# A hybrid SSD and stick-breaking trunk on one core: the key's split one step later, the last two attention units multiplied before either is added, and the form products behind the third sum

## The chip, the core and the metric

The kernel runs on one core of a Trainium2 chip. A core has a matrix engine (TensorE; PE in the rows, with PEld for its weight loads), a vector engine (DVE), an activation engine (ACT), a fourth engine for simple work on tensors (POOL), and a queue from which most transfers are issued (SP). Each engine executes its own instructions in order and waits on semaphores for the others. The metric is the device time in microseconds (us) of one launch.

## The reference, cut to what matters

The model is a two-layer trunk on 1024 tokens of width 1024, with 16 learned tokens in front (1040 in all). Layer 0 is a state-space mixer and a convolutional feed-forward network (FFN). Layer 1 is stick-breaking attention with 16 heads of 64, and another FFN.

```
h = concat(meta_tokens, x)
h = h + ssd_mixer(rmsnorm(h));   h = h + conv_ffn(rmsnorm(h))          # layer 0
k, v = split(rmsnorm(h) @ w_kv); q = rmsnorm(h) @ w_q
logits = q k^T / 8;  visible = s < t
log_keep = where(visible, log_sigmoid(-logits), 0)
later    = reverse_cumsum(log_keep) - log_keep
w        = exp(where(visible, log_sigmoid(logits) + later, -inf))
h = h + (w @ v) @ w_o;           h = h + conv_ffn(rmsnorm(h))          # layer 1
out = rmsnorm(h)[16:]
conv_ffn(u) = (silu(g) * val) @ w_down,   g, val = split(dwconv3(u @ w_up))
```

## The kernel before

**Numbers as two parts.** Every large product is made of three matmuls (L209, L210, L211): a float32 operand is split into a high part (rounded by a copy on ACT) and a low part (the difference, mostly on DVE or POOL). A "split" below is such a copy and such a difference.

**Attention.** Heads are worked in 8 pairs. A pair's keys, queries and values are projected (tile `pj`) in three token tiles of 348, 348 and 344. For a pair there are 18 steps n = 0 to 17, each a block of at most 116 queries (i, 0 to 8) against one tile of keys (jj). In the order of the code they are i = 0, 1, 2 with jj = 0 (n = 0 to 2); i = 3, 4, 5 with jj = 1, then 0 (n = 3 to 8); i = 6, 7, 8 with jj = 2, 1, 0 (n = 9 to 17). So step 9 is the first that reads key tile 2, and its logits are the first after step 3 that are only 116 columns wide.

A step does this. PE multiplies queries and keys (`lg`, L1653, into a tile of two PSUM banks of which there is one). ACT takes two sigmoids of it (`kp` L1654, `bt` L1655). DVE scans `kp` (L1664) and multiplies into `bt` (L1665). Two steps later PE transposes `bt` (`wT`, L1687), ACT copies that out (`wt`, L1693), and when a visit is complete PE multiplies it with the values (`po`, L1710); ACT and DVE split the result (L1713, L1714), and it goes to DRAM.

While pair p is in its steps, the projections of pair p+1 and the rest of pair p's own are spread over them by the table `halves` in `attention`: key tile 2 of the pair itself is projected in steps 4 and 5, key tile 0 of the next pair in steps 8 and 9, key tile 1 of the next in steps 14 and 15. `half` multiplies the finished key by its token factors on DVE at once (L1577) and returns a list of calls for the step after (`late`, then `todo`). For a key that call is `key`: the copy on ACT (L1588), the difference `klo` on DVE (L1589), and three transfers on SP (L1590 to L1592) that move halves of the two parts to other partitions, so that a query can meet both parts. PE, DVE, ACT and POOL execute the attention in the order in which the code issues it.

**The output projection** of the first 4 pairs begins in the last pair: units of 12 matmuls (`acc`), each followed by an add to the residual on DVE (L538). After the last step two units are taken from a two-bank tile (`both`, named `acc` too), the others from single banks.

**Entering an FFN.** `enter_ffn` finishes the residual, makes a factor per token (L993 to L999), and `forms` makes sums and differences of quarters of the normalised residual, split into parts: the products with the factors on DVE (L1091), differences on DVE (`ft`, L1115), the copies on ACT (`bh`, L1097) and the differences on DVE (`bl`, L1098). These are the operands of a product in 7 instead of 8 multiplications, `up`. Of the second half of the tokens the forms are made while `up` multiplies the first block of weights (b = 0) with the first half. In that block three sums are formed (L1237), the third being `add(z, z, u2)` at the end of the third step. Outside the attention a scheduler sets each engine's order from the dependencies and a simulated time, with some orders tied by hand through `behind`.

Of the kernel before, what the change touches and what calls it, by code (L numbers as in the profile page):

```python
# [105 lines left out]
class Trunk:  # L106
    def __init__(self, ctx, tc, a):
        self.tc, self.nc, self.a = tc, tc.nc, a
        nc = self.nc
        self.cp = ctx.enter_context(tc.tile_pool(name="cp", bufs=1))  # L110
        self.qp = ctx.enter_context(tc.tile_pool(name="qp", bufs=NQ))
        self.tmps = ctx.enter_context(tc.tile_pool(name="up", bufs=8))
        self.wp = ctx.enter_context(tc.tile_pool(name="wp", bufs=3))
        self.mp = ctx.enter_context(tc.tile_pool(name="mp", bufs=2, space=bass.MemoryType.PSUM))
        self.sp = ctx.enter_context(tc.tile_pool(name="sp", bufs=SMB, space=bass.MemoryType.PSUM))
        self.dp = ctx.enter_context(tc.tile_pool(name="dp", bufs=1, space=bass.MemoryType.DRAM))
        self.lp = None
        self.n = 0
        self.open = []
        self.hold = self.copy_tie = self.silu_tie = None  # L120
        self.consts()


# [404 lines left out]
    def accumulate(self, h, f, s0, n, w, ks, front=0, bank=None, base=0, new=False):  # L528

        ps = (bank or (self.ex if f % 3 == 2 else self.mm))("acc")  # L530
        c, o = slice(s0 - base, s0 - base + n), slice(front + s0, front + s0 + n)
        for i, (hi, lo) in enumerate(ks):
            wh, wl = w(i, f)
            self.mm3(ps[:, :n], wh, wl, hi[:, c], lo[:, c], i == 0, i == len(ks) - 1)
        if new:
            self.nc.vector.tensor_copy(h[f][:, o], ps[:, :n])
        else:
            self.nc.vector.tensor_tensor(h[f][:, o], h[f][:, o], ps[:, :n], op=ALU.add)  # L538

# [535 lines left out]
    def forms(self, layer, h, r, t, tiles, pool):  # L1075


        nc, gain, FN = self.nc, f"ffn_norm{layer}", FFN[layer].tile
        N, N2 = HB + FN, HB + 2 * FN
        K = range(KD // 2)  # L1080
        out, own, wide = tiles
        s = slice(2 * FN * t, 2 * FN * t + N2)

        new = slice(s.start + HB * t, s.stop)
        b1, b2 = [h[k][:, s] for k in K], [h[k + KD // 2][:, s] for k in K]
        b11, b12, b21, b22 = [[b[:, c] for b in rows] for rows in (b1, b2) for c in (slice(0, N), slice(FN, N2))]

        def product(ks, part):
            c = slice(new.start, s.start + N) if part == 0 else slice(s.start + N, new.stop)
            for k in ks:  # L1090
                nc.vector.scalar_tensor_tensor(h[k][:, c], h[k][:, c], self.par(gain, k), r[:, c], op0=ALU.mult, op1=ALU.mult)  # L1091

        last = [self.after_factors, None]

        def parts(hls, xs):
            for hl, x in zip(hls, xs):
                hi = nc.scalar.activation(hl[0], x, AF.Copy)  # L1097
                low = nc.vector.tensor_tensor(hl[1], x, hl[0].bitcast(F32), op=ALU.subtract)  # L1098
                if t:
                    self.behind(hi, last[0], "behind the factors and the form in front")  # L1100
                    self.behind(low, last[1], "behind the form in front")
                    last[:] = hi, low
            self.last_high, self.last_low = hi, low

        def form(i, xs):
            own(i)
            parts(out[i], xs)

        def columns(tiles, xs, c):
            return [tuple(x[:, c] for x in hl) for hl in tiles], [x[:, c] for x in xs]  # L1110

        def minus(xs, ys, place=None):
            place = place or [self.ft(pool)[:, :N] for _ in K]
            for o, x, y in zip(place, xs, ys):
                nc.vector.tensor_tensor(o, x, y, op=ALU.subtract)  # L1115
            return place

        product(K, 0)
        if t:
            product(range(KD // 2, KD), 0)  # L1120
            yield
            product(K, 1)
            yield
            t1 = minus(b12, b11)
            product(range(KD // 2, KD), 1)
            yield
            t2 = minus(b22, t1)
            form(0, b11)
            both = wide()
        else:  # L1130
            yield
            form(0, b11)
            product(range(KD // 2, KD), 0)
            yield
# [66 lines left out]
    def up(self, layer, w0, forms, rest, pool):  # L1201
# [8 lines left out]
        def block(b, t, w, late=None):  # L1210

            def product(i, ps, start=True):
                wh, wl, c0 = w[i]
                for k in range(KD // 2):
                    c = slice(c0 + k * P, c0 + k * P + P)
                    self.mm3(ps[:, :N], wh[:, c], wl[:, c], *forms[t][0][i][k], start and k == 0, k == KD // 2 - 1, not start, self.after_sums if late is not None and i and k == 0 else None)
                return ps

            def conv(x, i, c):
                o = self.tmp("c")
                self.conv(x, o[:, :FN], FN, 3, HB, lambda q: self.par(cw, (KF * i + b) * 3 + q), self.par(cb, KF * i + b), tie=None if late is None else self.first_low)
                if i == 0:
                    nc.scalar.activation(o[:, :FN], o[:, :FN], AF.Silu)
                return o

            def done(g, v, j):
                self.last_up = tt(g[:, :FN], g[:, :FN], v[:, :FN], op=ALU.mult)
                nc.sync.dma_start(d[b, :, FN * j : FN * j + FN], g[:, :FN])  # L1230

            def copy(ps):
                s = self.ft(pool)
                nc.scalar.activation(s[:, :N], ps[:, :N], AF.Copy)  # L1234
                return s

            add = lambda o, x, y: tt(o[:, :N], x[:, :N], y[:, :N], op=ALU.add)  # L1237
            x = product(0, self.mm("p"))
            p1 = copy(x)
            yield  # L1240
            y = product(2, self.sm("p"))
            add(y, y, p1)
            u2 = copy(y)
            yield
            z = product(3, (self.ex if next(turn) else self.lg)("p"))
            p5 = copy(z)
            add(z, z, u2)
            yield
            made = {}
            run = (lambda f: f()) if late is None else late.append  # L1250
            product(1, x, False)
            run(lambda: made.update(g0=conv(x, 0, 0)))
            yield
            u3 = copy(product(4, y, False))
            run(lambda: (add(p5, p5, u3), made.update(v1=conv(p5, 1, 1))))
            yield
            product(5, z, False)
            run(lambda: done(conv(z, 0, 1), made["v1"], 2 * t + 1))
            yield
            product(6, y, False)  # L1260
            run(lambda: done(made["g0"], conv(y, 1, 0), 2 * t))
            yield
# [252 lines left out]
    def heads(self, u, p, pool):  # L1515
# [4 lines left out]
        class Pair:  # L1520
# [38 lines left out]
            def half(me, kind, j, h, bank=None, parts=2):  # L1559
# [15 lines left out]
                t = self.tmp(kind)  # L1575
                if kind == "k":
                    nc.vector.tensor_tensor(t[:, :n], ps[:, :n], u[KD][:, o:e], op=ALU.mult)  # L1577
                    return [lambda: me.key(j, t)]
                nc.scalar.activation(t[:, :n], ps[:, :n], AF.Copy)
                me.late.append((j, t))  # L1580
                return []
# [137 lines left out]
    def attention(self, u, pool, hd):  # L1719
# [34 lines left out]
        for kind, j, bank in (("k", 0, self.mm), ("q", 0, self.mm), ("k", 1, self.sm), ("q", 1, self.ex)):  # L1754
            for h in range(2):
                for f in first.half(kind, j, h, bank):
                    f()
            if (kind, j) == ("k", 0):
                self.late_factors()
        self.token_factors(u[KD], pool)  # L1760
        for p in range(PAIRS):
            prev = None
            for n, (i, jj) in enumerate(steps):
# [14 lines left out]
                for own, pair in now.items():  # L1778
                    if p + 1 < PAIRS and (own, n) in halves:
                        late += pair.half(*halves[own, n])  # L1780
                for f in todo + chores[:1]:
                    f()
                del chores[:1]
                for own, pair in now.items():
# [4 lines left out]
        both = self.lg2("acc")  # L1789
        banks = iter([lambda s, a=a: both[:, a] for a in range(2)])  # L1790
        self.unit_bank = lambda s: next(banks, self.mm)(s)
        while turns or ready:
            next(behind)
            next(behind)
            flush(0)
        return od, behind

# [260 lines left out]
```

## Time and profile before

| | |
|---|---|
| three runs | 2851.83, 2857.06, 2860.83 us, median 2857.06 |
| the profiled execution | 2855.13 us, of which the span of instructions is 2853.3 |
| busy in the span | PE 2809.2, DVE 2065.4, ACT 1580.2, POOL 1578.6 us |
| attention, pair 0's first logits to the last add | about 1539 to 2061 us, some 65.2 us a pair |
| forms of the second half | about 838 to 862 us in layer 0, 2164 to 2191 us in layer 1 |
| mean granted clock of the matrix engine | 0.997 |

A row of the timeline has the start, the length, engine, line, operation, tiles (out <- in), shape and count, and in brackets the idle time of the engine just before it with what ended it. A row of waits has the waiting engine and line, the line waited for, the total, the count and the longest. A row of a window has its length, then for PE, PEld, DVE, ACT and POOL the busy time with the count of instructions, then the granted clock of the matrix engine, the busy share of the transfer engines and GB/s. Tiles' buffer numbers are left out in the profile.

### The profile page before, as it was taken

What the parts mean: (1) busy time and instruction counts of PE and PEld (TensorE: products, weight loads), DVE (VectorE), ACT (ScalarE), POOL (GpSimd) and SP (SyncE); (2) the same over time, 40 slices, a digit from 0 to 9 for tenths busy, and PEclk for the clock granted to TensorE, in tenths of its full rate; (3) what the DMA queues carried; (4) which work ended last, traced back from release to release, by engine and by line L of the source; (5) the groups of instructions that cost most, each with busy time, mean ns of one, the idle gap of its engine ahead of it and who ended that gap; (6) DMA issues with size and microseconds to landing.
All of it is one profiled execution on the core that took longest, in us unless ns stands there. A gap on an engine that the chain in (4) does not pass through costs nothing.

```text
span 2853.3 us, 56464 instructions
## 1 busy us (share of the span) xinstructions
PE 2809.2 (98%) x21251; PEld 2691.9 (94%) x21251; DVE 2065.4 (72%) x3936; ACT 1580.2 (55%) x3077; POOL 1578.6 (55%) x2144
## 2 busy tenths in 40 slices
PE   8999999999999999999999999999999999999998
PEld 7989999999999999999999999999899999999888
DVE  5676666668487676767886888888749676766776
ACT  5554554543256555555335777777536555555433
POOL 2366455553519888867763212112254888886881
PEclk9999999999999999999999999999999999999999
DMA  4333333343413222235142222222532222225331
GB/s 119 86 112 93 121 83 125 116 136 101 120 64 96 78 80 78 79 135 176 49 142 77 74 73 69 80 70 57 184 131 77 82 80 82 75 82 185 111 104 67
DMA packets 141740, 281.78 MB, mean 99 GB/s; under 512 B 16307, under 2 KB 71740, under 8 KB 141468
## 3 DMA queue, kind: packets, MB, share of 16 engines
q1 hardware_dynamic: 135844, 267.01, 29.8%
q0 software_dynamic: 2048, 6.49, 0.6%
q10 hardware_dynamic: 3576, 4.67, 0.5%
q8 instruction: 168, 2.75, 0.4%
q14 instruction: 104, 0.85, 0.1%
HBM read 207.79 MB, written 55.42 MB: 92 GB/s over the span
## 4 chain that ended last, share of the span: by engine, by line
PE 91%; DVE 4%; ACT 2%; POOL 1%; issue 1%; DMA 0%; SPq 0%; ACTq 0%; DVEq 0%; POOLq 0%
PE p L209 10%; PE p L210 10%; PE p L211 10%; PE acc L209 8%; PE acc L211 8%; PE acc L210 8%; PE pj L209 8%; PE pj L210 8%; PE pj L211 8%; PE po L1710 3%; PE lg L1653 2%; PE wT L1687 2%; PE y L810 1%; PE S L799 1%; PE y L812 1%; PE ms L1069 1%
## 5 line engine op out<-in xcount | busy, mean ns | idle before, releaser
L102 POOL TENSOR_TENSOR wl<-w,wh 128x256 fp32r<-128x256 f32 x760 | 678.9, 923 | 352.2 <-ACT wh L196 225.4
L209 PE MATMUL pj<-uh,wh 128*128 128x348 f32 (+2 forms) x1536 | 500.4, 326 | 2.1 <-DVE xbc L339 1.4
L210 PE MATMUL pj<-ul,wh 128*128 128x348 f32 (+2 forms) x1536 | 494.9, 322 | 0.8 <-DVE ul L320 0.8
L211 PE MATMUL pj<-uh,wl 128*128 128x348 f32 (+2 forms) x1536 | 492.0, 320 | 0.0
L209 PE MATMUL p<-bh,fh 128*128 128x262 f32 (+1 forms) x1408 | 400.9, 285 | 3.9 <-DVE p L1237 3.7
L211 PE MATMUL p<-bh,fl 128*128 128x262 f32 (+1 forms) x1408 | 401.0, 285 | 0.9 <-POOL fl L102 0.9
L210 PE MATMUL p<-bl,fh 128*128 128x262 f32 (+1 forms) x1408 | 399.2, 284 | 0.0
L102 POOL TENSOR_TENSOR fl<-x,fh 128x256 fp32r<-128x256 f32 x352 | 264.3, 783 | 186.8 <-ACT fh L1174 160.9
L210 PE MATMUL p<-bl,wh 128*128 128x262 f32 (+1 forms) x1040 | 295.6, 284 | 1.1 <-DVE bl L1098 1.1
L209 PE MATMUL p<-bh,wh 128*128 128x262 f32 (+1 forms) x1040 | 295.3, 284 | 0.4 <-ACT ft L1234 0.4
L211 PE MATMUL p<-bh,wl 128*128 128x262 f32 (+1 forms) x1040 | 294.1, 283 | 0.0
L209 PEld LDWEIGHTS pj<-uh,wh 128*128 128x128 f32 x1536 | 288.7, 188 | 4.5 <-ACT xbc L336 1.7
L210 PEld LDWEIGHTS pj<-ul,wh 128*128 128x128 f32 x1536 | 289.2, 188 | 2.4 <-DVE ul L320 1.4
L211 PEld LDWEIGHTS pj<-uh,wl 128*128 128x128 f32 x1536 | 288.7, 188 | 0.1
L339 DVE SCALAR_TENSOR_TENSOR c<-p,params,c 128x260 f32<-128x260 f32 (+1 forms) x528 | 248.4, 480 | 54.7 <-ACT c L336 48.3
L209 PEld LDWEIGHTS p<-bh,fh 128*128 128x128 f32 x1408 | 268.0, 191 | 4.7 <-DVE p L1237 4.1
L211 PEld LDWEIGHTS p<-bh,fl 128*128 128x128 f32 x1408 | 267.1, 190 | 1.6 <-POOL fl L102 1.5
L210 PEld LDWEIGHTS p<-bl,fh 128*128 128x128 f32 x1408 | 267.8, 190 | 0.5 <-DVE bl L1098 0.4
L1234 ACT ACTIVATE ft<-p 128x262 f32<-128x262 f32 (+1 forms) x352 | 133.2, 382 | 179.9 <-DVE p L1237 110.1
L210 PE MATMUL acc<-gl,wh 128*128 128x260 f32 (+1 forms) x672 | 214.2, 320 | 0.0
L211 PE MATMUL acc<-gh,wl 128*128 128x260 f32 (+1 forms) x672 | 213.2, 319 | 0.0
L209 PE MATMUL acc<-gh,wh 128*128 128x260 f32 (+1 forms) x672 | 210.8, 320 | 0.1
(336 smaller groups left out, 7690.6 us busy)
## 6 DMA issues: line engine op xcount, KB each, us to landing
w<-in_w_up SPq DMA_DIRECT2D x88, 512.0 KB
w<-in_w_down SPq DMA_DIRECT2D x44, 512.0 KB
w<-in_w_in SPq DMA_DIRECT2D x40, 512.0 KB
E<-ea_d SPq DMA_DIRECT2D x32, 464.0 KB
D<-acs_d SPq DMA_DIRECT2D x32, 420.5 KB
g<-c SPq DMA_DIRECT2D x88, 130.0 KB
g<-c SPq DMA_DIRECT2D x88, 128.0 KB
b<-g SPq DMA_DIRECT2D x16, 520.0 KB
```

What stands on the lines that cost most here:

```text
L102: done.append(eng.tensor_tensor(out[:, c], x[:, c], y[:, c], op=op))
L209: self.behind(mm(out, wh, uh, start=first, stop=False, skip_group_check=joins), tie, "behind the sums of squares")
L210: mm(out, wh, ul, start=False, stop=False, skip_group_check=joins)
L211: self.last_mm = mm(out, wl, uh, start=False, stop=last, skip_group_check=joins)
L339: ins = nc.vector.scalar_tensor_tensor(out, ps[:, o + i : o + i + n], wcol(i), out, op0=ALU.mult, op1=ALU.add)
L799: nc.tensor.matmul(ps, bk[:n], xde[:n].rearrange("p h d -> p (h d)"), start=True, stop=True)
L810: nc.tensor.matmul(y, xdt[:n, i, :], dk[:, i, :], start=True, stop=c == 0)
L812: nc.tensor.matmul(y, state[:, i, :], ce[:, i, :], start=False, stop=True)
L1234: nc.scalar.activation(s[:, :N], ps[:, :N], AF.Copy)
L1653: nc.tensor.matmul(ps[:nt, a, :m], part[:, c0 : c0 + nt], ks[a][:, s0 : s0 + m], start=x == 0, stop=x == 1)
L1687: nc.tensor.transpose(pt[:ns, x * CB : x * CB + nt], bt[:nt, a, x * CB : x * CB + ns], self.ident[:nt, :nt])
L1710: nc.tensor.matmul(po[64 * a : 64 * a + 64, t0:n], v[: CH[c][1], c, 64 * a : 64 * a + 64], wt[a][q][: CH[c][1], r, t0:n], start=x == 0, st ...
```

## The change

Three edits.

1. In `half`, the call that a key returns gives back another call instead of doing the work, and the loop over steps appends what a call returns to `late`. So `key` (ACT copy, DVE difference, three transfers) is done one step later: in step 7 for key tile 2 of the pair's own (step 3 in the last pair), in step 11 and in step 17 for the next pair's tiles 0 and 1. The token-factor product L1577 stays.
2. In the loop that ends the attention, the adds of the first two units are collected and issued after both units' matmuls.
3. In the second half's `forms`, the products of the rows K..2K with the last factors are issued one step later, and tied behind the third sum of `up`, which now remembers it; since the order of the scheduler is then weighed anew, the first half of these products, which have no tie, and the following differences move with them.

```diff
@@ accumulate
+        elif self.adds is not None:
+            self.adds.append(lambda: self.nc.vector.tensor_tensor(h[f][:, o], h[f][:, o], ps[:, :n], op=ALU.add))
@@ forms
-        def product(ks, part):
+        def product(ks, part, tie=None):
             c = slice(new.start, s.start + N) if part == 0 else slice(s.start + N, new.stop)
             for k in ks:
-                nc.vector.scalar_tensor_tensor(h[k][:, c], ...)
+                ins = nc.vector.scalar_tensor_tensor(h[k][:, c], ...)
+                self.behind(ins, tie, "behind the third sum")
@@
             product(K, 1)
             yield
+            yield
+            product(range(KD // 2, KD), 1, self.third_sum)
             t1 = minus(b12, b11)
-            product(range(KD // 2, KD), 1)
-            yield
             t2 = minus(b22, t1)
@@ up, block
-            add(z, z, u2)
+            self.third_sum = add(z, z, u2)
@@ heads, half
-                    return [lambda: me.key(j, t)]
+                    return [lambda: [lambda: me.key(j, t)]]
@@ attention
-                for f in todo + chores[:1]:
+                for f in todo:
+                    late += f() or []
+                for f in chores[:1]:
                     f()
@@
         self.unit_bank = lambda s: next(banks, self.mm)(s)
+        self.adds = []
         while turns or ready:
             next(behind)
             next(behind)
+            for f in self.adds or ():
+                f()
+            self.adds = None
             flush(0)
```

Three places show what this does to the order. After the change the lines of the code are 2 to 3 higher (L1589 becomes L1592, L1664 L1667, L1665 L1668).

DVE in pair 1, from the token-factor product of key tile 2 (step 5) to the scan of step 8; `klo` is the key's difference, the two scans of 116x349 with a `bt` behind each are steps 6 and 7. Before:

```order
L1577 TENSOR_TENSOR k_18725<-pj_18663,r_17778 128x344
L1555 SCALAR_TENSOR_TENSOR wl_18728<-w_2359_18686,params,wh_18727 128x128 x4
L1664 SCALAR_TENSOR_TENSOR kp_18747<-kp_18747,kp_18696,one 116x349 x2
L1665 TENSOR_TENSOR bt_18748<-bt_18748,kp_18747 116x2x348
L1589 TENSOR_TENSOR klo_18773<-k_18725,k_18288 128x344
L1555 SCALAR_TENSOR_TENSOR wl_18728<-w_2359_18686,params,wh_18727 128x128 x4
L1714 TENSOR_TENSOR o_18788<-po_18789,o_18787 128x348
L1664 SCALAR_TENSOR_TENSOR kp_18810<-kp_18810,one 116x349 x2
L1665 TENSOR_TENSOR bt_18811<-bt_18811,kp_18810 116x2x348
L1664 SCALAR_TENSOR_TENSOR kp_18853<-kp_18853,kp_18810,one 116x349 x2
```

After the change, the same stretch:

```order
L1580 TENSOR_TENSOR k_18725<-pj_18663,r_17778 128x344
L1558 SCALAR_TENSOR_TENSOR wl_18728<-w_2359_18686,params,wh_18727 128x128 x4
L1667 SCALAR_TENSOR_TENSOR kp_18747<-kp_18747,kp_18696,one 116x349 x2
L1668 TENSOR_TENSOR bt_18748<-bt_18748,kp_18747 116x2x348
L1558 SCALAR_TENSOR_TENSOR wl_18728<-w_2359_18686,params,wh_18727 128x128 x4
L1717 TENSOR_TENSOR o_18782<-po_18783,o_18781 128x348
L1667 SCALAR_TENSOR_TENSOR kp_18804<-kp_18804,one 116x349 x2
L1668 TENSOR_TENSOR bt_18805<-bt_18805,kp_18804 116x2x348
L1592 TENSOR_TENSOR klo_18835<-k_18725,k_18288 128x344
L1667 SCALAR_TENSOR_TENSOR kp_18853<-kp_18853,kp_18804,one 116x349 x2
```

The difference moved from behind the `bt` of step 6 to behind the `bt` of step 7; four other groups of rows (a weight's low parts, an output's low part, the scan and `bt` of step 7) are now ahead of it. In SP's queue the three transfers of this key, which stood ahead of an output's store and a load of 512 KB of weights, now stand behind both.

PE behind the last step, in the second of the two units (24 matmuls write `acc_25466`, 12 for each unit) and in the third unit (`acc_25537`), with the waits:

```order
 L210 MATMUL acc_25466<-o_24904,wh_25222 128x256
 L211 MATMUL acc_25466<-o_24904,wl_25223 128x256
-L209 MATMUL acc_25466<-o_25069,wh_25222 128x256 [waits DVE_49]
+L209 MATMUL acc_25466<-o_25069,wh_25222 128x256
 L210 MATMUL acc_25466<-o_25069,wh_25222 128x256
 L211 MATMUL acc_25466<-o_25069,wl_25223 128x256
```

The second unit no longer waits for DVE; the third and the fourth unit, some 50 instructions on, now have a wait on DVE. The order of the instructions is the same on PE and on DVE.

DVE in layer 0, behind the end of the second half's factors (L999); `p` is the third sum, the rows on `h` are products with the factors, of which there are eight in a row, and the rows on `ft` are differences. Before, the last three of the eight and what follows:

```order
L1091 SCALAR_TENSOR_TENSOR h_7083<-h_7083,params,r_8313 128x260
L1091 SCALAR_TENSOR_TENSOR h_7134<-h_7134,params,r_8313 128x260
L1091 SCALAR_TENSOR_TENSOR h_7185<-h_7185,params,r_8313 128x260
L1115 TENSOR_TENSOR ft_9132<-h_6828 128x262
L1115 TENSOR_TENSOR ft_9133<-h_6879 128x262
L1115 TENSOR_TENSOR ft_9134<-h_6930 128x262
L1115 TENSOR_TENSOR ft_9135<-h_6981 128x262
L1237 TENSOR_TENSOR p_9144<-p_9144,ft_9130 128x262
L1115 TENSOR_TENSOR ft_9160<-h_7032,ft_9132 128x262
```

After, from the end of the factors on:

```order
L1001 SCALAR_TENSOR_TENSOR r_8313<-y_9072,r_8313 128x260
L1240 TENSOR_TENSOR p_9132<-p_9132,ft_9130 128x262
L1093 SCALAR_TENSOR_TENSOR h_6828<-h_6828,params,r_8313 128x260
L1093 SCALAR_TENSOR_TENSOR h_6879<-h_6879,params,r_8313 128x260
L1093 SCALAR_TENSOR_TENSOR h_6930<-h_6930,params,r_8313 128x260
```

The third sum moved ahead of the eight products and of four differences, to the row behind the factors' end. Layer 1 moves alike. Further on, in the second block of weights, the scheduler also changed the order of a few matmuls, copies and POOL differences in both layers.

More of the change, by code (lines that the diff above doesn't have):

```diff
@@ L119, in __init__ @@
         self.open = []
-        self.hold = self.copy_tie = self.silu_tie = None
+        self.adds = self.hold = self.copy_tie = self.silu_tie = None
         self.consts()
@@ L1086, in forms @@
         b11, b12, b21, b22 = [[b[:, c] for b in rows] for rows in (b1, b2) for c in (slice(0, N), slice(FN, N2))]
-        def product(ks, part):
+        def product(ks, part, tie=None):
             c = slice(new.start, s.start + N) if part == 0 else slice(s.start + N, new.stop)
             for k in ks:
-                nc.vector.scalar_tensor_tensor(h[k][:, c], h[k][:, c], self.par(gain, k), r[:, c], op0=ALU.mult, op1=ALU.mult)
+                ins = nc.vector.scalar_tensor_tensor(h[k][:, c], h[k][:, c], self.par(gain, k), r[:, c], op0=ALU.mult, op1=ALU.mult)
+                self.behind(ins, tie, "behind the third sum")
         last = [self.after_factors, None]
@@ L1756, in attention @@
                 for f in first.half(kind, j, h, bank):
-                    f()
+                    for g in f() or ():
+                        g()
             if (kind, j) == ("k", 0):
```

## The prediction, on record before the run

> **What bounds the kernel now.** I read the busy times and the chain first, then the matrix engine's waits, then the timeline of each stretch that the change touches.
>
> ```profile
> PE 2809.2 (98%) x21251; PEld 2691.9 (94%) x21251; DVE 2065.4 (72%) x3936; ACT 1580.2 (55%) x3077; POOL 1578.6 (55%) x2144
> PE 91%; DVE 4%; ACT 2%; POOL 1%; issue 1%; DMA 0%; SPq 0%; ACTq 0%; DVEq 0%; POOLq 0%
> PE lg L1653 <- ACT bt L1655: 6.3, 11, 0.8
> PE acc L209 <- DVE h L538: 4.3, 2, 3.3
> PE p L209 <- DVE p L1237: 3.7, 2, 1.9
> PE wT L1687 <- DVE v L1620: 1.8, 4, 1.0
> ```
>
> The matrix engine (PE) is busy for 98% of the span and makes 91% of the chain. No other engine can be made to matter except by making PE idle, and a microsecond of PE idle is lost for good unless a later idle one goes away. So the change is worth what it does to PE's waits, of which these four groups (16.1 us) are the ones near its edits. The three edits aim at the first three: ACT's delay in the attention, the add between two units, and the third sum of the FFN's entry.
>
> An idle stretch can cost more than itself. The two waits on the third sum are alike in length, the wait on the add is the longest of the stretch:
>
> ```profile
> 843.70 0.39 PE L209 MATMUL p<-bh,fh 128*128 128x262 f32 x1 [1.86 <-DVE p L1237]
> 846.00:848.00 2.00, 2.00 (x11) 2.00 (x11) 2.00 (x8) 1.74 (x5) 0.00 (x0) 0.50 0.00 0
> 2169.69 0.39 PE L209 MATMUL p<-bh,fh 128*128 128x258 f32 x1 [1.83 <-DVE p L1237]
> 2170.00:2172.00 2.00, 2.00 (x19) 2.00 (x18) 2.00 (x7) 2.00 (x6) 0.00 (x0) 1.00 0.00 0
> 2061.03 0.58 PE L209 MATMUL acc<-o,wh 128*128 128x256 f32 x1 [3.31 <-DVE h L538]
> 2061.00:2063.00 2.00, 1.97 (x9) 1.97 (x10) 0.00 (x0) 0.00 (x0) 0.00 (x0) 0.50 0.97 349
> 2065.00:2067.00 2.00, 2.00 (x16) 1.31 (x14) 0.00 (x0) 0.00 (x0) 0.00 (x0) 0.52 1.04 395
> 2067.00:2069.00 2.00, 2.00 (x22) 1.38 (x19) 0.01 (x1) 0.38 (x2) 0.00 (x0) 1.00 1.04 399
> ```
>
> Behind 1.86 us of idle the granted clock is 0.50 (by the matmuls' spacing from 844.9 to 848.3, 3.4 us), behind 1.83 us it stays 1.00, behind 3.31 us it is 0.50 until about 2067. Half clock on a busy PE loses half its length: 1.7, 0 and (2067.0 - 2061.0)/2 = 3.0 us. The mean of the three is 1.6 us; the bounds are 0 and 3.0.
>
> **The units (second edit), the surest term.** PE multiplies the first unit until 2057.6 and then idles until DVE, whose queue holds a scan and `bt` of the last step ahead of the add, has added it; the two units share a two-bank tile. With both multiplied first, nothing holds the second. The wait that now stands at the third unit is for these adds:
>
> ```profile
> 2059.18 1.12 DVE L1665 TENSOR_TENSOR bt<-bt,kp 112x696 f32<-112x696 f32 x1
> 2060.23 0.74 DVE L538 TENSOR_TENSOR h<-h,acc 128x258 f32<-128x258 f32 x2
> ```
>
> PE comes to the third unit after the second (12 matmuls at some 0.12 us, 1.45 us), the output's 32 matmuls (3.1 us) and six transposes (0.5 us), so at 2057.6 + 5.05 = 2062.65. DVE begins its adds at 2060.23 as before and is through by about 2061.5. No new wait, and no half clock: -(3.4 + 3.0) = **-6.4 us**, the 3.4 being the idle time as PE's issue sees it (2057.6 to 2061.0). Bounds: -3.4 if the clock drops all the same, -6.4.
>
> **The keys (first edit).** What it removes is this, once in each of the seven pairs that prepare another (steps 10 to 12):
>
> ```profile
> 1642.29 0.49 ACT L1588 ACTIVATE k<-k 128x348 fp32r<-128x348 f32 x1 [0.79 <-DVE k L1577]
> 1646.15 0.68 PE L1653 MATMUL lg<-k,qs 128*116 128x232 f32 x4 [0.65 <-ACT bt L1655]
> PE lg L1653 <- ACT bt L1655: 4.5, 7, 0.7
> PE wT L1687 <- DVE v L1620: 0.8, 3, 0.3
> ```
>
> ACT stands 0.79 us before the key's copy because DVE has not made its product; the sigmoids behind it come late, and PE waits 0.65 us at step 12. One step later the product has long been made and the copy (0.38 us by the spacing of ACT's rows) fits. The last two rows are PE's waits from 1570 to 2000 us: seven of the first kind, 4.5 us, and three on the values, 0.8 us. I take both away, **-5.3 us**.
>
> What it adds is at step 9, which reads key tile 2. Pair 1, before:
>
> ```profile
> 1621.56 1.78 DVE L1664 TENSOR_TENSOR_SCAN kp<-kp,kp,one 116x349 f32<-116x349 f32 x2 [1.41 <-ACT kp L1654]
> 1631.50 0.51 DVE L1589 TENSOR_TENSOR klo<-k,k 128x344 fp32r<-128x344 f32 x1
> 1631.93 1.39 DVE L1555 SCALAR_TENSOR_TENSOR wl<-w,params,wh 128x128 fp32r<-128x128 f32 x4
> 1635.42 0.88 DVE L1665 TENSOR_TENSOR bt<-bt,kp 116x696 f32<-116x696 f32 x1
> 1636.22 1.77 DVE L1664 TENSOR_TENSOR_SCAN kp<-kp,kp,one 116x349 f32<-116x349 f32 x2
> 1632.04 0.48 SPq L1591 DMA_DIRECT2D k<-klo  x1
> 1632.62 0.55 SPq L1592 DMA_DIRECT2D k<-klo  x1
> 1634.00:1634.25 0.25, 0.25 (x3) 0.25 (x3) 0.25 (x1) 0.25 (x1) 0.00 (x0) 1.00 0.88 187
> 1634.25:1634.50 0.25, 0.25 (x4) 0.25 (x3) 0.25 (x2) 0.25 (x2) 0.00 (x0) 1.00 0.09 22
> 1635.74 0.60 PE L1653 MATMUL lg<-k,qs 128*116 128x116 f32 x4
> ```
>
> The difference starts at 1631.50, the two transfers from it are issued 0.54 and 1.12 us later, and their packets end at about 1634.25, 1.63 us after the second issue. PE's step 9 comes at 1635.74: 1.5 us to spare. After the change the difference stands behind the `bt` of step 7. That ends, by the start of the next row, at 1636.22; without the difference in front (0.43 us to the next row) at 1635.79. So the transfers are issued at 1636.33 and 1636.91. How soon PE may start behind them has two bounds: the packets' end, +1.63, and the shortest distance at which PE is seen not to wait, in pair 0:
>
> ```profile
> 1567.66 0.55 SPq L1592 DMA_DIRECT2D k<-klo  x1
> 1570.29 0.59 PE L1653 MATMUL lg<-k,qs 128*116 128x116 f32 x4
> ```
>
> That is +2.63. So step 9 starts between 1638.54 and 1639.54 instead of 1635.74: PE stands **2.8 to 3.8 us**. I take 3.0, nearer the packets' end, because 2.63 only says that no wait was left. On PE all is queued behind these four matmuls: the values' transposes, the projections, the next `wT`.
>
> Could DVE come earlier? From the scan at 1621.56, for which it had waited 1.41 us on ACT, thus on PE's step 4, until 1636.22 its rows follow without a gap, and the edit takes only 0.43 us from them. Each pair starts this chain anew, so a stall in one pair does not buy slack for the next. SP's queue, where an output's store (issued at 1633.78) and 512 KB of weights (1634.20) now stand ahead, is passed well before 1636.33, though the weights' traffic may press towards the upper bound. The other keys have time: tile 0 of the next pair is read seven steps after its split, tile 1 four, tile 2 of the last pair six.
>
> Seven pairs: 7 x 3.0 = **+21.0 us**, and for the clock 7 x 1.6 = **+11.2 us** (a wait of 3.0 us is nearer to the 3.31 us row with its 3.0 than to the two short ones, of which one cost nothing; where in time the clock is judged seems to decide, so I stay with the mean). Bounds +19.6 and, with 3.8 and 3.0, +47.6.
>
> The Trainium skill, page "TensorE: Matmul & The Clock Gate", section "Part 1: The HAM clock gate (the 'warmup' mystery)", says the array falls to the half-rate state after at least one idle window of some 3.4 us. By that rule no stall of 3.0 us would bring it down and the 11.2 us would be nil; the trace disagrees at 846 us, where 1.86 us of idle was enough.
>
> **The forms (third edit).** In layer 0 the third sum now stands ahead of eight products and four differences, so the 1.86 us wait goes, and the half clock behind it. But DVE is what PE meets next:
>
> ```profile
> 838.64 3.29 DVE L1091 SCALAR_TENSOR_TENSOR h<-h,params,r 128x260 f32<-128x260 f32 x8
> 843.21 0.44 DVE L1237 TENSOR_TENSOR p<-p,ft 128x262 f32<-128x262 f32 x1
> 845.94 1.80 DVE L1098 TENSOR_TENSOR bl<-ft,bh 128x262 fp32r<-128x262 f32 x5
> 851.82 0.39 PE L210 MATMUL p<-bl,wh 128*128 128x262 f32 x1 [0.36 <-DVE bl L1098]
> 2177.70 0.39 PE L210 MATMUL p<-bl,wh 128*128 128x258 f32 x1 [0.70 <-DVE bl L1098]
> ```
>
> DVE executes without a gap from 836 to 862 us and has as much to do as before; behind the place where the sum stood its times are the same. PE, 3.6 us earlier, waits at `bl` (845.94 and later), and at 851.82 both orders meet. Layer 1 meets at 2177.70. I take **0**. Bounds: -5.4 (1.86 + 1.7 + 1.83, if all of it lasts) and +3.4 (a half-clock stretch of 1.7 in each layer from waits newly run together). The reordering in the second block lies inside these.
>
> **The sum.** -6.4 - 5.3 + 21.0 + 11.2 + 0 = +20.5 us on the profiled 2855.1, so 2875.6. The median of the runs is 1.9 us above the profiled execution: **2877.5 us**, slower by 0.7%. All low ends: 2857.0 - 6.4 - 5.3 + 19.6 - 5.4 = 2859.5. All high ends: 2857.0 - 3.4 - 5.3 + 47.6 + 3.4 = 2899.3.
>
> **Rivals.**
>
> *The keys land in time (the other side).* Then only the gains are left, -11.7: 2845.4. For it: the waits it removes are in the trace. It decides at step 9: PE would not wait if the difference started by 1635.74 - 1.12 - 1.63 = 1633.0, and it starts at 1635.79 by a DVE chain without gaps. 0.13.
>
> *The stalls come, the clock does not drop,* as behind the 1.83 us wait in layer 1: +9.3, 2866.3. Against it: two of three waits of that size or more did drop it. By the page's rule named above this is the case. 0.13.
>
> *The stalls are half as long,* because PE itself reaches step 9 later or the transfers land sooner than the rows show: 7 x 1.7 = +11.9 against -11.7, about 2857. Nothing in the trace shows which of the two. 0.08.
>
> *The forecast*, stalls with clock losses: 0.66.
>
> **How the numbers follow.** A measurement of this kernel tells 0.3% (8.6 us) from nothing: faster is below 2848.5, slower above 2865.6. Faster: the first rival, but for its edge, 0.11. Slower: nearly all of the forecast and half of the second rival, 0.70. The same: the rest, 0.19. The range 2859 to 2894 holds the forecast but for its upper end, the second rival, and leaves out the first.
>
> **What would show it.** In the profile after, seven waits of PE at `lg` (116 columns wide, one a pair, 65 us apart and growing to about 69) on a transfer, 2.8 to 3.8 us each, where before there was none, and a granted clock below 1 in the windows behind most of them; no waits at step 12; no 3.3 us wait at `acc`; no wait on the third sum, but new or longer ones on `bl`, with PE at the same place by 852 and 2178. I am wrong if the seven waits are absent or short; if the FFN's entries end sooner, the forms are mis-sized; if the stalls are there with the clock at 1.00, the clock is.

## The result, and the profile after

| | before | after |
|---|---|---|
| median of the first comparison | 2857.06 us | 2886.86 us (2885.80 to 2892.25, five runs) |
| ratio | | 1.0118, 95% interval 1.0106 to 1.0130 |
| profiled execution, its span | 2855.13, 2853.3 us | 2892.25, 2890.3 us |
| granted clock, mean | 0.997 | 0.991 |

The change makes the kernel slower by 1.2%. Against the forecast of 2877.5 us (2859 to 2894) this is the forecast's case, 9.4 us above its point. In the later comparisons the median of the kernel before is 2854.2 to 2854.9 us, and the change, measured once more in experiment 10, is 34.9 us above it. The profiled span grew by 37.0 us, more than the 29.8 us between the medians: the profiled execution of the change is the slowest of its five. From the page of the changed kernel, busy times and chain of waits:

```profile
PE 2824.0 (98%) x21251; PEld 2706.7 (94%) x21251; DVE 2080.2 (72%) x3936; ACT 1580.7 (55%) x3077; POOL 1555.9 (54%) x2144
PE 89%; DVE 5%; ACT 2%; DMA 2%; POOL 2%; issue 1%; ACTq 0%; SPq 0%; DVEq 0%; POOLq 0%
```

PE makes the same 21251 matmuls and is busy 14.8 us longer, so some run at a lower clock. DMA is now 2% of the chain, where it was 0%. Those of PE's waits after the change that bear on its edits (waiting tile and line, what was waited for, total, count, longest):

```profile
PE lg L1656 <- DMA k<-klo: 28.0, 7, 4.4
PE p L209 <- ACT c L1228: 3.0, 1, 3.0
PE lg L1656 <- ACT bt L1658: 1.9, 4, 0.8
PE p L209 <- ACT bh L1100: 1.8, 2, 0.9
PE p L210 <- DVE bl L1101: 1.4, 2, 0.7
PE acc L209 <- DVE h L540: 1.0, 1, 1.0
PE wT L1690 <- DVE v L1623: 1.0, 1, 1.0
```

The first row is new: seven waits on the key's transfer, 28.0 us. The waits on `bt` went from 6.3 to 1.9 us, on the add from 4.3 to 1.0, and the 3.7 us on the third sum are gone; `bh` and more of `bl` have come in their place. The second row is new and was not foreseen. The attention as one window, from the first logits to the last, before and then after (columns as in the prediction's windows):

```profile
1538.80:2052.10 513.30, 505.25 (x3836) 467.48 (x3834) 432.53 (x763) 383.26 (x903) 108.71 (x295) 1.00 0.28 81
1538.90:2090.60 551.70, 520.75 (x3836) 483.97 (x3834) 439.25 (x763) 384.22 (x903) 93.60 (x295) 0.96 0.26 75
```

For the same 3836 matmuls PE was busy 505.25 us and is now busy 520.75: 15.5 us of half clock. Its idle time (window less busy) went from 8.1 to 31.0 us: 28.0 of stalls less the 5.2 taken away at `bt` and at the values. Together the attention is 38.4 us longer. From the end of the last logits to the end of the last `ms` matmul ahead of layer 1's FFN the program takes 101.4 instead of 107.7 us, the gain of the second edit; from there to the end 697.4 instead of 692.6 us, 4.8 more. 38.4 - 6.3 + 4.8 is 36.9 of the 37.0 us. (The expectations below put the last part at 5.9 us.)

Pair 1 after the change, rows of DVE, SP and PE around step 9:

```profile
1641.12 0.89 DVE L1668 TENSOR_TENSOR bt<-bt,kp 116x696 f32<-116x696 f32 x1
1641.92 0.51 DVE L1592 TENSOR_TENSOR klo<-k,k 128x344 fp32r<-128x344 f32 x1
1639.05 0.34 SPq L1537 DMA_DIRECT2D w<-in_w_kv  x1
1639.96 0.48 SPq L1593 DMA_DIRECT2D k<-k  x1
1642.46 0.48 SPq L1594 DMA_DIRECT2D k<-klo  x1
1643.73 0.46 SPq L1595 DMA_DIRECT2D k<-klo  x1
1645.99 0.99 PE L1656 MATMUL lg<-k,qs 128*116 128x116 f32 x4 [3.97 <-DMA k<-klo]
```

PE is ready at 1642.02 (1645.99 - 3.97), 0.10 us after the difference has begun. The second transfer follows the difference by 0.54 us as predicted, but the third comes 1.27 us behind the second, not 0.58, and PE starts 2.26 us behind the third. The seven stalls are 4.28, 3.97, 3.91, 4.40, 4.01, 4.13 and 3.34 us long. Behind each the granted clock is 0.50, in some for one stretch, in others for two. Pair 1, then pair 0:

```profile
1647.00:1649.00 2.00, 2.00 (x9) 2.00 (x9) 0.88 (x3) 1.92 (x6) 0.81 (x4) 0.50 0.03 8
1650.00:1652.00 2.00, 2.00 (x16) 1.98 (x16) 1.57 (x5) 1.19 (x3) 0.00 (x0) 1.00 0.00 0
1576.00:1578.00 2.00, 2.00 (x9) 2.00 (x8) 0.95 (x3) 1.96 (x6) 0.81 (x4) 0.50 0.00 0
1579.00:1581.00 2.00, 2.00 (x11) 1.92 (x11) 0.90 (x3) 0.33 (x1) 0.00 (x0) 0.52 0.00 0
```

### The profile page after: what moved, and what is told of

Its sections match the earlier page's. It is cut to its first block, busy times and chain, and to the rows that moved or that the text cites. A ratio compares the mean times of both kernels' runs of the same rounds, so it can differ in the third digit from the quotient of the medians.

```text
span 2890.3 us, 56476 instructions
## 1 busy us (share of the span) xinstructions
PE 2824.0 (98%) x21251; PEld 2706.7 (94%) x21251; DVE 2080.2 (72%) x3936; ACT 1580.7 (55%) x3077; POOL 1555.9 (54%) x2144
## 4 chain that ended last, share of the span: by engine, by line
PE 89%; DVE 5%; ACT 2%; DMA 2%; POOL 2%; issue 1%; ACTq 0%; SPq 0%; DVEq 0%; POOLq 0%
PE p L209 9%; PE p L211 9%; PE p L210 9%; PE acc L209 8%; PE acc L211 8%; PE acc L210 8%; PE pj L209 8%; PE pj L210 8%; PE pj L211 8%; PE po L1713 2%; PE lg L1656 2%; PE wT L1690 2%; PE y L812 1%; PE S L801 1%; DVE kp L1667 1%
## 5 line engine op out<-in xcount | busy, mean ns | idle before, releaser
L1662 POOL TENSOR_SCALAR_AFFINE_SELECT kp<-kp 116x232 f32<-116x232 f32 (+1 forms) x72 | 39.3, 546 | 318.5 <-ACT kp L1657 311.9
```

The costliest lines, as they stand in the source:

```text
L1662: nc.gpsimd.affine_select(out=t[:nt, :, c0 : c0 + nt], in_=t[:nt, :, c0 : c0 + nt], compare_op=ALU.is_gt, fill=fill, base=0, pattern=[[0, ...
```

## The experiments

Each experiment is a kernel compared with the kernel before on one chip. In the table the attention is measured from the first to the last logits of the profiled execution, and PE's idle time in it is that stretch less PE's busy time.

| kernel | ratio to before, 95% interval | attention, us | PE idle in it | PE busy in it |
|---|---|---|---|---|
| before | 1 | 513.3 | 8.1 | 505.2 |
| the change | 1.0118 (1.0106 to 1.0130) | 551.6 | 31.0 | 520.7 |
| 1 second edit alone | 0.9980 (0.9971 to 0.9989) | 513.2 | 8.0 | 505.2 |
| 2 key tile 2 alone | 1.0137 (1.0121 to 1.0152) | 551.7 | 31.1 | 520.6 |
| 3 first edit alone | 1.0134 (1.0117 to 1.0151) | 550.4 | 30.9 | 519.5 |
| 4 third edit alone | 1.0003 (0.9993 to 1.0012) | 513.3 | 8.1 | 505.2 |
| 5 other key tiles, second edit | 0.9969 (0.9956 to 0.9981) | 509.2 | 4.5 | 504.7 |
| 6 key 2 projected earlier | 0.9971 (0.9960 to 0.9982) | 509.8 | 3.9 | 505.9 |
| 7 key 2 a step later still | 1.0168 (1.0150 to 1.0187) | 564.0 | 46.7 | 517.4 |
| 8 first transfer on ACT's queue | 1.0113 (1.0099 to 1.0127) | 550.3 | 30.9 | 519.3 |
| 9 weights behind the transfers | 1.0043 (1.0029 to 1.0056) | 530.3 | 18.4 | 511.9 |
| 10 the change again | 1.0120 (1.0104 to 1.0137) | 550.3 | 31.7 | 518.6 |

My theory: the loss is the distance from key tile 2's split to step 9, in stalls and their half clock. The rivals: the edits make it together, or the moved order in layer 1's FFN does, or the third transfer is late for another reason than the weights ahead of it. A "stall" below is one of PE's waits at step 9.

**1 to 4: the edits one by one.**

Experiment 1 is the second edit alone (the `adds` list, no other line).

> The second edit alone. Theory (the +29.8 us between the two medians is the late key tile 2, less a true gain of the units edit, plus a loss in layer 1's second block that comes with a moved order there): the 3.3 us wait at `acc` goes, the half clock behind it too, nothing behind it moves; 6.3 us less than before, about 2851. Rival (the units edit itself makes the loss that layer 1's feed-forward shows, because it reaches it earlier): the 6.3 us are given back there, about 2857.

Measured: 2848.41 against 2854.17 us, 5.8 us less. The wait at `acc` is down from 4.3 to 1.0 us, and of the 6.3 us expected at most half a microsecond is given back in the FFN. The theory holds.

Experiment 2 splits only key tile 2 later:

```diff
-                    return [lambda: me.key(j, t)]
+                    return [lambda: [lambda: me.key(j, t)]] if j == 2 else [lambda: me.key(j, t)]
```

> The first edit for key tile 2 alone; tiles 0 and 1 of the next pair are split when they were before. Theory (the stall at step 9 is this tile's transfers): seven waits of 4 us on a transfer at `lg`, 28 us, half clock behind them 15.5 us, and the waits at step 12 stay since their cause (a copy of tile 0 or 1) is where it was: +43.5 us, about 2900. Rival (the split of all three tiles one step later crowds the two engines that make the values, and tile 2 alone would be in time or nearly so): under +15 us, below 2872.

Measured: 2893.18 us, 39.0 more than before, where 43.5 was expected. Two of its groups of waits, then the next key's copy on ACT and the product it needs on DVE, in step 11 of pair 1:

```profile
PE lg L1653 <- DMA k<-klo: 28.2, 7, 4.4
PE lg L1653 <- ACT bt L1655: 1.8, 4, 0.8
1653.46 0.49 ACT L1588 ACTIVATE k<-k 128x348 fp32r<-128x348 f32 x1
1650.33 0.52 DVE L1577 TENSOR_TENSOR k<-pj,r 128x348 f32<-128x348 f32 x1 [1.26 <-PE pj L211]
```

The stalls are there with tile 2 alone, and the whole of the attention's loss with them. That the waits at step 12 stay was a miss: they went too, although tile 0's copy is where it was. The copy no longer stands, since DVE made the product 3.1 us ahead of it: while PE stood at step 9, DVE emptied its queue and then even waited for PE. In the presence of the stall, moving the other two tiles is worth at most the 1.3 us between 551.7 and 550.4.

Experiment 3 is the first edit alone, all three tiles.

> The first edit alone, all tiles. Theory: the 43.5 us of the stalls and their clock less the 5.3 us of the waits at step 12, +38 us; the last stretch of layer 1 has almost the moved order of the whole change here, so up to +5.9 us more: 2895 to 2901. Rival (the three edits make the stall together, for instance because the units edit moves the queues): less than +30 us, below 2887.

Measured: 2892.06 us, 37.9 more. The theory's 38 (the expected times, from 2895 on, were counted from 2857 us, and the kernel before had 2854.17 here); the seven stalls are again 28.0 us, so the other edits have no part in them.

Experiment 4 is the third edit alone.

> The third edit alone. It leaves the order in layer 1's second block nearly as before (two rows of ACT change places). Theory: nothing, as predicted: the wait on the third sum goes and waits on the forms come, PE meets the same times behind them: 2857 plus or minus 2. Rival (the third edit is what costs 5.9 us in layer 1's feed-forward): 2863. Second rival (the wait on the third sum and its half clock are a true gain): 2851.6 to 2855.

Measured: 2855.09 against 2854.17 us, no change that can be told. PE's wait of 3.7 us on the third sum is gone, and 1.8 us on `bh` stands there instead. A wait of 1.6 us on ACT's `c` further on is of the kind that experiment 10 is about.

**5 and 6: the same change without the stall.**

Experiment 5 keeps tile 2 where it was and moves the other two, with the second edit:

```diff
-                    return [lambda: me.key(j, t)]
+                    return [lambda: [lambda: me.key(j, t)]] if j < 2 else [lambda: me.key(j, t)]
```

> The second edit, and the first for tiles 0 and 1 of the next pair alone; tile 2 is split where it was. Tests what took the waits at step 12 away. In the run of tile 2 alone (e2) these went as well, though the copies of tiles 0 and 1 stood where they did before. Theory one (as in the prediction: the copy of tile 0 or 1 that stands before its product delays the sigmoids): the seven waits go here too, without a stall, 4.5 to 5.3 us less than the units edit alone, about 2844 to 2846. Theory two (ACT runs late for the whole of a pair, and only PE's standing still at step 9 lets it catch up): the waits stay or move, 2849 to 2851. A loss of up to 5.9 us in layer 1's feed-forward may come with the moved order there; it is told apart in the profile.

Measured: 2844.53 against 2854.44 us, 9.9 less. Its row of waits at step 12's kind of place:

```profile
PE lg L1655 <- ACT bt L1657: 1.8, 4, 0.8
```

The seven waits went without a stall, and the attention is 4.1 us shorter: theory one. So the copy that stood before its product was a true cause, and a stall elsewhere was another way to be rid of it.

Experiment 6 is the whole change with query and key tile 2 exchanged in the table of projections:

```diff
-            (0, 0, "v", 1), (0, 2, "q", 2), (0, 4, "k", 2), (0, 6, "v", 2),
+            (0, 0, "v", 1), (0, 2, "k", 2), (0, 4, "q", 2), (0, 6, "v", 2),
```

> The whole change, with key tile 2 projected at steps 2 and 3 and query tile 2 at 4 and 5, so that the key's split stands two steps sooner (behind step 5) and its transfers are there before step 9. Theory (the stall is the distance from the split to step 9): no wait on a transfer at `lg`, clock full, 2845 to 2852. Rival (the additional step itself, or what DVE does there, makes PE stand): seven waits of over 2 us remain, over 2870. The query, later now, could bring a wait of its own.

Measured: 2845.56 us, 8.9 less than before. The difference, the last transfer and PE's step 9 in pair 1:

```profile
1625.28 0.51 DVE L1592 TENSOR_TENSOR klo<-k,k 128x344 fp32r<-128x344 f32 x1
1626.37 0.56 SPq L1595 DMA_DIRECT2D k<-klo  x1
1634.67 0.60 PE L1656 MATMUL lg<-k,qs 128*116 128x116 f32 x4
```

The last transfer is issued 8.3 us ahead of step 9, no wait on it is left in any pair, and the mean clock in the attention is 1.00. This and experiment 5 are the fastest versions, 0.3% below the kernel before; between the two no difference can be told. Experiment 1, with the second edit alone, beats both kernels too, by 0.2%.

**7: a step more.**

```diff
+                    return [lambda: [lambda: [lambda: me.key(j, t)]]] if j == 2 else [lambda: [lambda: me.key(j, t)]]
```

> The whole change, with key tile 2 split one step later still. Theory (the distance from the split to step 9 is what PE stands): the stall grows by about the time of the step between, which is DVE's to the next `bt`, 3 to 5 us; seven of 7 to 9 us, 2910 to 2935. Rival (PE stands for something else that ends at a fixed time, as the 512 KB of weights): stalls of about 4 us as before, 2887.

Measured: 2902.76 us; seven stalls, 43.2 us, thus 6.2 us each: longer by 2.2 us, where 3 to 5 was expected, and the time is below the 2910 us expected at least. Pair 1:

```profile
1650.17 0.51 DVE L1592 TENSOR_TENSOR klo<-k,k 128x344 fp32r<-128x344 f32 x1
1650.71 0.48 SPq L1594 DMA_DIRECT2D k<-klo  x1
1651.28 0.55 SPq L1595 DMA_DIRECT2D k<-klo  x1
1653.81 1.00 PE L1656 MATMUL lg<-k,qs 128*116 128x116 f32 x4 [6.25 <-DMA k<-klo]
```

PE is ready at 1647.56, and the difference begins 2.6 us behind that, instead of 0.1 ahead: one scan and one `bt`. But the third transfer is issued 0.57 us behind the second again, which gives 0.7 back. Both rows speak for the distance, and against a fixed time.

**8 and 9: why 4.0 and not 3.0 us.** The third transfer overwrites what the first reads and so waits for it. In the changed kernel's last stall, 256 KB of weights stand ahead of the transfers instead of 512:

```profile
1992.05 0.34 SPq L1828 DMA_DIRECT2D w<-in_w_o_f  x1
1995.46 0.48 SPq L1594 DMA_DIRECT2D k<-klo  x1
1996.03 0.55 SPq L1595 DMA_DIRECT2D k<-klo  x1
```

Here the third comes 0.57 us behind the second, and the stall is 3.34 us. Experiment 8 takes the first transfer out of SP's queue:

```diff
+                e = nc.scalar if j == 2 else nc.sync
-                nc.sync.dma_start(y[64:, c].bitcast(F32), x[64:, c].bitcast(F32))
+                e.dma_start(y[64:, c].bitcast(F32), x[64:, c].bitcast(F32))
```

> The whole change, with one thing moved: the first of tile 2's three transfers, which copies the rounded key, is issued from ACT's queue behind its copy instead of from SP's. The third transfer overwrites what the first reads, and so waits for its end. Theory (the 1.0 us by which the stall is longer than predicted is the first transfer standing behind 512 KB of weights in SP's queue): the last issue comes 0.6 us behind the second instead of 1.27, stalls of 3.3 us instead of 4.0; 5 us less than the whole change, or up to 12 less if the clock comes back a window sooner: 2875 to 2882. Rival (the transfers run late because the rings are busy with the weights, whoever issues): 2887.

Measured: 2885.75 us, stalls of 28.0 us, as before this edit. The three issues in pair 1, then the queues' packets (queue, packets, MB, share of the transfer engines) from 1638 to 1640 us, and from 1640 to 1641, where q10 is ACT's queue:

```profile
1637.04 0.49 ACTq L1594 DMA_DIRECT2D k<-k  x1
1640.12 0.48 SPq L1595 DMA_DIRECT2D k<-klo  x1
1641.39 0.48 SPq L1596 DMA_DIRECT2D k<-klo  x1
...
q1 hardware_dynamic: 190, 0.54, 82.0%
...
q1 hardware_dynamic: 80, 0.09, 24.9%
q10 hardware_dynamic: 80, 0.09, 24.5%
```

The first transfer was issued 3.1 us ahead of the second and had no packet before 1640 us, when nearly all of the other queue's weights and about half of an output's store, issued 0.1 us behind it, were through (0.54 MB from 1638 to 1640); the third still came 1.27 us behind the second. My theory of the queue fell: it is not the place in the queue but the transfer engines that are taken. The Trainium skill, page "DMA: Bandwidth & Descriptors", section "Issuing engines are not separate DMA queues", says that transfers run on the same engines whoever issues them; these rows agree. That such transfers interleave, as it also says, they show only from 1640 us on, where packets of both queues come; until then the small one had none.

Experiment 9 issues the weights one step later, behind the transfers:

```diff
-        loads = {(-1, 4): "k", (-1, 7): "q", (-1, 9): "v"}
+        loads = {(-1, 5): "k", (-1, 7): "q", (-1, 9): "v"}
```

> The whole change, with the 512 KB load of the next pair's key weights issued one step later, so that it stands behind key tile 2's three transfers instead of ahead of them. In the run with the first transfer on ACT's queue (e8) that transfer's packets still came only when the weights' were through, and the third was issued 1.27 us behind the second as before. In the seventh stall of the changed kernel, where only 256 KB stand ahead, it is 0.57 us, and the stall 3.34 us instead of 3.9 to 4.4. Theory (the transfer engines are taken by the 512 KB, whichever queue issues): 0.6 us between second and third issue in all seven, stalls of 3.0 to 3.4 us, 22 to 24 us in all instead of 28; 5 us less than the whole change, 2881, or less still if the clock comes back a window sooner. Rival (the third transfer waits for its semaphore or for the second): stalls of 4.0 us as before. The weights now land later, so a wait of ACT or PE for them may come: its own row would show it.

Measured: 2867.99 us, 21.8 less than the whole change in the same comparison (experiment 10), where 5 or somewhat more was expected. Its two groups of waits at step 9, and pair 1:

```profile
PE lg L1656 <- ACT wt L1696: 13.0, 6, 2.2
PE lg L1656 <- DMA k<-klo: 2.5, 1, 2.5
...
1634.53 0.79 ACT L1696 ACTIVATE wt<-wT 116x348 f32<-116x348 f32 x2
1634.99 0.51 DVE L1592 TENSOR_TENSOR klo<-k,k 128x344 fp32r<-128x344 f32 x1
1636.10 0.55 SPq L1595 DMA_DIRECT2D k<-klo  x1
1636.74 0.54 SPq L1537 DMA_DIRECT2D w<-in_w_kv  x1
1638.30 0.59 PE L1656 MATMUL lg<-k,qs 128*116 128x116 f32 x4 [2.17 <-ACT wt L1696]
```

Six waits are put down to ACT's `wt`, but that had ended at 1635.32, long before PE was ready at 1636.13. PE starts 2.20 us behind the third issue (2.26 after the change, 2.53 in experiment 7), so this is the same wait on the transfer under another name. The third follows the second (1635.53) by 0.57 us, as the theory has it (0.57 to 0.60 in six pairs, 0.92 in one). The stall is 2.2 us, shorter than the 3.0 to 3.4 expected, since a second thing came with the edit: part of the next weights' low parts, DVE's work, moved behind the split as well, and the difference now begins 1.14 us ahead of PE's arrival instead of 0.10. So 0.7 us of the 1.8 are the issue and 1.0 DVE's queue.

**10: the change once more,** without an edit.

> The changed kernel as it is, for a second profile. In the first one, DVE's `ft` product at 2234 us took 5.96 us for two instead of 1.63 as in e8, which has the same order there, and PE then waited 3.0 us for ACT's `c`. Theory (a chance event: that product, with both operands in SBUF, stands until POOL's run of operations ends): it stands elsewhere or nowhere in the second profile, and the runs spread over two values about 5 us apart. Rival (the order in layer 1's second block brings it): the same wait at the same place.

Measured: 2889.83 us, runs from 2886.82 to 2891.88. In the first profile, the rows behind PE's 3.0 us wait in layer 1:

```profile
2234.27 5.96 DVE L1240 TENSOR_TENSOR ft<-ft,ft 128x258 f32<-128x258 f32 x2
2236.78 1.45 POOL L102 TENSOR_TENSOR x<-w 128x256 f32<-128x256 f32 x2
2238.16 1.45 POOL L102 TENSOR_TENSOR x<-x,w 128x256 f32<-128x256 f32 x2
2239.93 1.10 ACT L336 ACTIVATE c<-ft,params 128x256 f32<-128x256 f32 x2 [4.84 <-DVE ft L1240]
2245.75 0.36 PE L209 MATMUL p<-bh,fh 128*128 128x258 f32 x1 [3.01 <-ACT c L1228]
```

In the second, the same DVE row and no wait of PE:

```profile
2233.57 1.64 DVE L1240 TENSOR_TENSOR ft<-ft,ft 128x258 f32<-128x258 f32 x2
```

So the 4.8 us that the first profile lost from the last `ms` matmul to the end are not the change's: the second profiled execution has a span of 2884.8 us, 5.5 us less, and takes 692.7 us from that matmul to the end, like the kernel before (692.6). The theory's first half is shown (it stands in some executions), its reason only argued, below.

## Why the prediction was right, and where it was not

- **That PE stands at step 9, seven times, once a pair:** right, and for the reason given, as experiments 2, 6 and 7 show. The difference began 16.23 us behind the `lg` of step 4 (1625.69), where the prediction's chain had 16.15. Pairs are 70.6 us apart, not 69.
- **How long: 3.0 us, bounds 2.8 to 3.8.** Mis-sized: 4.0 on average, above the bound, 7.0 us in all. In pair 1, 0.69 of the missing 0.97 us is the third issue at 1.27 instead of 0.58 us behind the second, 0.43 is PE's start at 2.26 instead of 1.83 us behind it, and 0.15 goes the other way. The sentence that failed is that SP's queue "is passed well before": its issues are, but the packets of the 512 KB are not, and the third transfer waits for the first one's.
- **Clock, 7 x 1.6 = 11.2 us:** mis-sized; 15.5 us, 2.2 a stall, inside the bounds of 0 and 3.0. The second rival (clock stays) is out, and with it the rule of the Trainium skill, page "TensorE: Matmul & The Clock Gate", section "Part 1: The HAM clock gate (the 'warmup' mystery)", that it takes an idle window of 3.4 us: experiment 9 has half clock behind 2.17 us.
- **Step 12, -5.3 us:** the size was right (5.2 us less idle time at `bt` and at the values; 4.1 us of attention in experiment 5). Its reason, that the other key tiles' copies move, holds where there is no stall; in experiment 2, where those copies stay, the stall alone removes the same waits.
- **The units, -6.4 us:** right; 5.8 us in experiment 1, 6.3 us in the profile after.
- **The forms, 0:** right, +0.9 us with an interval around nothing in experiment 4. PE waits at `bh` and `bl` instead of the third sum.
- **The first rival's 2845.4 us** (keys in time) is what experiment 6 measures when the keys are in time: 2845.56. That the two agree so closely is luck: the gain is 8.9 us against the 2854.44 of that comparison, not 11.7 against 2857.06.
- **The sum:** from +20.5 to +37.0 us between the two profiles: +7.0 stalls, +4.3 clock, +0.1 units, +4.8 layer 1, and 0.3 elsewhere. The first two are the prediction's own errors; the fourth comes and goes. The stalls lie outside their own bounds, and the total is inside the range all the same because a stall and its clock were allowed up to 6.8 us together (4.6 in the forecast) and took 6.2.

## What to carry to other kernels

Count slack for a moved step at its reader, transfers and their ordering among themselves included, and ask what else the transfer engines carry at that moment: here a transfer of 86 KB waited for the packets of 512 KB of weights from either queue (experiment 8). A gain and a stall in one loop need not add, since the stall let the other engines catch up (experiment 2). When several edits come together, run each alone: here the second edit was good, the third harmless, and a part of the first (the other key tiles) worth keeping.

## What the runs showed that I had not expected

**The clock is judged on a fixed grid.** At the change's seven stalls half clock lasts 3.41 us (twice) or 6.83 (five times) by the trace's clock records, and its ends lie whole multiples of 3.41 us apart (from 1649.2 in pair 1 to 1720.9 in pair 2, 21 of them). Two stalls of like length in experiment 9 are the 2.17 us in pair 1, shown above, and the first row here, in pair 4; below it are the windows of 2 us some 3 us behind each:

```profile
1842.33 0.59 PE L1656 MATMUL lg<-k,qs 128*116 128x116 f32 x4 [2.13 <-ACT wt L1696]
1641.00:1643.00 2.00, 2.00 (x11) 1.92 (x10) 1.56 (x6) 0.00 (x0) 0.00 (x0) 0.55 0.00 0
1845.00:1847.00 2.00, 2.00 (x17) 2.00 (x15) 1.90 (x7) 1.34 (x3) 0.00 (x0) 1.00 0.00 0
```

Up to the next pair's step 9 PE was busy 65.8 us behind the first and 64.3 behind the second, so half clock cost 1.5 us; of the seven, five had half clock like the first. What tells them apart is how the grid divides the stall. In pair 1 half clock begins at 1639.4, so the grid's stretch ahead of that, from 1636.0, holds the whole stall (1636.1 to 1638.3). In pair 4, 59 stretches later, the grid cuts the stall (1840.2 to 1842.3) at 1840.8 into 0.6 and 1.5 us. Over experiment 9's seven stalls the larger part was 1.8 to 2.4 us in the five with half clock and at most 1.6 in the two without. It would explain the kernel before as well: its 1.86 us lay whole in the stretch ahead of 844.9, and its 1.83 us were cut into 1.45 and 0.38 (half clock began later, at 2179.55, which puts the cut at 2169.3). It is not the whole rule, since that half clock at 2179.55 came behind only 1.1 us of idle time in its stretch; what else counts stays open.

A longer stall does not cost more clock: experiment 7's, 6.2 us long, cost 12.2 us in all, the change's 15.5. More of the half clock then passes while PE still stands: in pair 1 it begins at 1650.4, 3.4 us ahead of PE's start, and after the change at 1645.8, 0.2 us ahead.

**A vector product can stand still, perhaps for POOL.** The `ft` product has both operands in SBUF and mostly takes 0.4 to 1.1 us. In some executions one took 3.7 to 5.9 us, three times in the first profile of the change. There each ended within 0.3 us behind the end of a run of POOL operations without a gap (at 2234.27 the first of the row's two products did, at 2239.9). The Trainium skill, page "SBUF — State Buffer", section "SBUF: two separate sides", says that such an operation and one of POOL lock each other out for an instruction; if that is the reason here, DVE was locked out for several of POOL's in a row, five to eight in these three. That was not tested. The first profile, where PE waits for what follows, is 4.8 us longer in that part than the second, and the runs of the change lie near 2886 and near 2891; that these products are what parts the runs was not shown.
